# Group B's norm ahead of the output projection, z_b blocks last, and one accumulation for all 32 k-tiles

## The chip, the cores and the metric

One core of a Trainium2 chip. The metric is the device time of one launch in microseconds (us), the median of the runs shown. The engines are named as in the profile: PE is TensorE (matmuls), PEld its weight loads, DVE is VectorE, ACT ScalarE, POOL GpSimd, SP SyncE, which only issues transfers (DMAs).

## The reference: one encoder layer with two kinds of heads

256 tokens, 2048 channels, all in fp32:

```
hn = rmsnorm(x, norm_w)
q, v, f_fwd, f_bwd, z_a, b_gate, c_gate, h_b, z_b = split(hn @ w_in)        # 9 x 2048 columns
o_a = head_rmsnorm(hgrn2_forward(...) + hgrn2_backward(...)) * silu(z_a)     # group A
y_b = b_gate * conv3(c_gate * h_b)                                          # group B
o_b = rmsnorm(y_b, conv_norm_w) * silu(z_b)
h   = x + concat(o_a, o_b) @ w_out                                          # 4096 x 2048
h   = h + (p @ w_ple) * sigmoid(h @ w_ple_gate)
out = rmsnorm(h, final_norm_w)
```

The norm of o_b has one scale per token, taken from all 2048 channels of y_b. z_b is also scaled by the input norm before its silu.

## The kernel before

**Matmuls.** An fp32 product is made from two rounded halves of each operand: x = hi + lo. Three matmuls (hi·hi, hi·lo, lo·hi) give one product. Every weight block is split on the chip: ScalarE rounds it (L121), VectorE subtracts to get the rest (L122). For blocks of w_in with the tokens as moving operand, hi and lo of the activations lie side by side, and a matmul of 512 columns and one of 256 do the three (L437, L435): 64 matmuls a block, `gemm_in`.

**The weight stream.** `Stream` holds the weight blocks in the order of use. A block is loaded by SyncE into a raw buffer (three of `rawp`; from a place in w_out on, a tile named `early` is the fourth), and split into parts, each in one of five `spl` buffers. `get(i)` makes parts up to three ahead of the one asked for, with high priority. A scheduler orders each engine's instructions by priority and by when it holds them ready; all engines then run their own list in order.

**Seven products for eight.** Two pairs of output columns and two k-tiles form a 2x2 block product: eight tile products, or seven with sums of weights and sums of activations (`half`, L565 and the lines around it: `three` is one product of three matmuls). Seven need four extra PSUM banks beside the four main ones and a combination on VectorE when the banks are done. The weight sums come from one of two places. `add_own` makes them in the raw buffer with three VectorE adds (L83). `add_sums` reads them ready-made from DRAM: SyncE has copied weights to `sums` (`prepare`), and GpSimd has added to them there with accumulating transfers (L345 from w_out, then two steps L349), issued one by one at set ticks by `pumps`. A tick is a place in the matmul stream; `at(n, f)` runs f in the program n ticks later.

**Group B.** Group A takes the first half of the span. Then for i = 0..7 (256 channels each): c_gate and h_b blocks (for i = 0, 1 one by one with `gemm_in`; for i = 2, 4, 6 both columns of two i at once in `gemm_ch`, where pairs 2 and 4 of eight are seven products), then b_gate, the convolution and y_b, its square into `ysum`, then z_b, its sigmoid, the product o = y_b·silu(z_b)·conv_norm_w (without the norm's token scale) and the split into `mixb`. Late entries of group A's mixed tiles are transposed after the last z_b block (`turn(6)`, `turn(7)`), and `norm_b` gets the scale `rb` per token there: two matmuls of `ysum` against a column of ones (L1035).

**w_out.** Two halves of 1024 output columns (u = 0, 1). For each, one pass over the 16 k-tiles of group A (`mixa`) and one over the 16 of group B (`mixb`). A pass has eight pairs in the order 0, 1, 2, 3, 6, 4, 5, 7; pairs 2, 3, 4 and 5 are seven products with sums from DRAM. Each pass has its own main and extra banks (psg and psm in turn), its own combination into `hh` (which holds the residual), and the group B passes are scaled by `rb` in that addition (`add_h`). Then h is transposed (`h_transposed`) for the gate projection.

## Time and profile before

| what | before |
|---|---|
| median of 3 runs | 1108.23 us (1108.08 to 1108.48) |
| the profiled execution | 1108.31 us, span 1106.6 us |
| granted TensorE clock | 0.998 |
| DMA | 260.43 MB, mean 235 GB/s |

The profile is of one execution. Its span is a little shorter than the execution's time. A line of the timeline gives the start in us, the duration, the engine, the line of the kernel, what is written and read, and in brackets the idle time before it and what ended it. Matmuls overlap, so their pace is read from starts. An fp32 matmul that is not split shows as more than one record. A row of the table of windows gives the window, its length, the engine's busy time in it, the count, the granted clock, the DMA share and GB/s. "DMA to landing" is the time from a transfer's issue to its last byte (min/median/max of those asked for).

### The profile page before, as it was taken

The numbers are of one execution on the slowest core, as the hardware profiler recorded it, in microseconds if no ns is written. First come the engines' busy times: TensorE is split into PE (matmuls) and PEld (weight loads), VectorE is DVE, ScalarE is ACT, GpSimd is POOL, SyncE is SP. The second block draws the span as 40 slices with busy tenths as digits, with TensorE's granted clock in tenths as the row PEclk, the third lists the DMA queues.
The fourth block names the chain that finished last, engine by engine and source line by source line (L and its number), as shares of the span: only waits on it lengthen the run. The fifth ranks groups of instructions, "written<-read, shape, count | busy, mean of one in ns | idle before, by whom it ended". The sixth has DMA issues, their size and how long they took to land.

```text
span 1106.6 us, 16633 instructions
## 1 busy us (share of the span) xinstructions
PE 1096.3 (99%) x6269; PEld 936.9 (85%) x6269; DVE 892.6 (81%) x1164; ACT 685.8 (62%) x943; POOL 249.2 (23%) x203
## 2 busy tenths in 40 slices
PE   9999999999999999999999999999999999999996
PEld 8888888888888888888888888888888888888886
DVE  7798588996889778997877798789778888887673
ACT  6696577667876697575554455455447565565562
POOL 1144215205530535053430130121031000000101
PEclk9999999999999999999999999999999999999999
DMA  9886995588747874757989568577567888887542
GB/s 345 324 275 205 281 301 188 167 297 229 259 159 249 276 235 153 232 197 207 252 219 290 164 210 255 161 241 222 196 209 283 294 309 285 278 314 252 190 133 77
DMA packets 83248, 260.43 MB, mean 235 GB/s; under 512 B 8160, under 2 KB 23904, under 8 KB 68704
## 3 DMA queue, kind: packets, MB, share of 16 engines
q1 hardware_dynamic: 73920, 242.25, 62.9%
q0 software_dynamic: 8960, 16.78, 9.7%
q8 instruction: 49, 0.80, 0.3%
q10 hardware_dynamic: 288, 0.34, 0.1%
q14 instruction: 31, 0.25, 0.1%
HBM read 257.25 MB, written 35.65 MB: 265 GB/s over the span
## 4 chain that ended last, share of the span: by engine, by line
PE 98%; DVE 1%; ACT 0%; DMA 0%; issue 0%; DVEq 0%; SPq 0%; ACTq 0%
PE a L437 29%; PE a L435 15%; PE ach L565 3%; PE ach L566 3%; PE ach L564 3%; PE avz L566 3%; PE avz L564 3%; PE avz L565 3%; PE pg L1072 3%; PE pg L1073 3%; PE pg L1071 3%; PE pa L564 2%; PE pa L566 2%; PE pa L565 2%; PE a L456 1%; PE a L458 1%
## 5 line engine op out<-in xcount | busy, mean ns | idle before, releaser
L122 DVE TENSOR_TENSOR spl<-raw,spl 128x1024 fp32r<-128x1024 f32 (+2 forms) x431 | 517.5, 1215 | 132.1 <-ACT spl L121 123.9
L121 ACT CAST spl<-raw 128x1024 fp32r<-128x1024 f32 (+2 forms) x431 | 424.4, 995 | 262.8 <-PE a L435 58.8
L437 PE MATMUL a<-xs,spl 128*128 128x512 f32 x1408 | 483.8, 395 | 0.0
L435 PE MATMUL a<-xs,spl 128*128 128x256 f32 x1408 | 376.5, 278 | 0.0
L437 PEld LDWEIGHTS a<-xs,spl 128*128 128x128 f32 x1408 | 260.0, 188 | 55.4
L435 PEld LDWEIGHTS a<-xs,spl 128*128 128x128 f32 x1408 | 262.5, 188 | 5.6
L1188 POOL TENSOR_TENSOR hh<-hh,fw 128x512 f32<-128x512 f32 (+1 forms) x9 | 11.0, 1227 | 251.4 <-ACT gt L1187 248.8
L565 PE MATMUL ach<-spl,xs 128*128 128x512 f32 x156 | 60.8, 390 | 0.5 <-DVE spl L122 0.5
L564 PE MATMUL ach<-spl,xs 128*128 128x512 f32 x156 | 60.7, 389 | 0.0
L566 PE MATMUL ach<-spl,xs 128*128 128x512 f32 x156 | 60.7, 389 | 0.0
L564 PE MATMUL avz<-spl,xs 128*128 128x512 f32 x138 | 54.0, 391 | 0.0
L566 PE MATMUL avz<-spl,xs 128*128 128x512 f32 x138 | 53.7, 389 | 0.0
L565 PE MATMUL avz<-spl,xs 128*128 128x512 f32 x138 | 53.7, 389 | 0.0
L989 POOL TENSOR_TENSOR cg<-cg,bg 128x512 f32<-128x512 f32 x8 | 11.2, 1405 | 182.3 <-DVE bg L504 182.3
L503 ACT COPY r<-a 128x256 f32<-128x256 f32 x88 | 31.5, 368 | 30.3 <-PE a L435 30.2
L1071 PE MATMUL pg<-spl,ht 128*128 128x512 f32 (+1 forms) x120 | 45.2, 377 | 0.0
L737 POOL TENSOR_TENSOR qc<-pf,ge 128x256 f32<-128x256 f32 x16 | 21.0, 1316 | 107.0 <-ACT dd L727 92.1
L1072 PE MATMUL pg<-spl,ht 128*128 128x512 f32 (+1 forms) x120 | 45.0, 375 | 0.0
L1073 PE MATMUL pg<-spl,ht 128*128 128x512 f32 (+1 forms) x120 | 45.0, 375 | 0.0
L83 DVE TENSOR_TENSOR raw<-raw 128x512 f32<-128x512 f32 (+1 forms) x45 | 43.2, 959 | 0.9
L122 DVE TENSOR_TENSOR spl<-early,spl 128x1024 fp32r<-128x1024 f32 (+1 forms) x29 | 32.8, 1147 | 9.6 <-ACT spl L121 9.1
L121 ACT CAST spl<-early 128x1024 fp32r<-128x1024 f32 (+1 forms) x29 | 28.6, 990 | 18.5 <-PE pb_y L566 7.5
(378 smaller groups left out, 1893.9 us busy)
## 6 DMA issues: line engine op xcount, KB each, us to landing
raw<-in_w_in_dram SPq DMA_DIRECT2D x82, 1024.0 KB, 6.0
raw<-in_w_in_dram SPq DMA_DIRECT2D x196, 256.0 KB, 4.1
raw<-in_w_out_dram SPq DMA_DIRECT2D x36, 512.0 KB, 5.0
sums<-in_w_out_dram SPq DMA_DIRECT2D x32, 512.0 KB, 8.2
raw<-in_w_in_dram SPq DMA_DIRECT2D x26, 512.0 KB, 5.8
raw<-sums SPq DMA_DIRECT2D x13, 1024.0 KB, 5.8
raw<-in_w_gate_dram SPq DMA_DIRECT2D x9, 1024.0 KB, 5.5
sums<-in_w_out_dram POOLq DMA_DIRECT2D x16, 512.0 KB, 11.0
```

The source lines that it names most:

```text
L83: self.nc.vector.tensor_tensor(out=out, in0=out, in1=other, op=ALU.add)
L121: self.nc.scalar.copy(out=v[:, :, 0], in_=r)
L122: self.nc.vector.tensor_tensor(out=v[:, :, 1], in0=r, in1=v[:, :, 0], op=ALU.subtract)
L435: pe.matmul(a[:, :T], lhsT=lhsT, rhs=xs[:, kt, 0, :], start=False, stop=(kt == NKT - 1))
L437: pe.matmul(a, lhsT=lhsT, rhs=xs[:, kt, :, :].rearrange("p s n -> p (s n)"), start=(kt == 0), stop=False)
L503: act.copy(out=r, in_=acc[m][:, 1, :])
L564: pe.matmul(acc, lhsT=ah, rhs=w[:, 0], start=start, stop=False)
L565: pe.matmul(acc, lhsT=ah, rhs=w[:, 1], start=False, stop=False)
L566: pe.matmul(acc, lhsT=al, rhs=w[:, 0], start=False, stop=stop)
L1071: pe.matmul(acc[m], lhsT=lh, rhs=wh, start=(kt == 0), stop=False)
L1072: pe.matmul(acc[m], lhsT=lh, rhs=wl, start=False, stop=False)
L1073: pe.matmul(acc[m], lhsT=ll, rhs=wh, start=False, stop=(kt == nk - 1))
```

## The change

- w_in's blocks come in another order: c and h for i = 0, 1; b_gate of both; then for i = 2, 4, 6 the c/h pair and two b_gate blocks; and all eight z_b blocks at the end.
- y_b is kept for all i. After the last, `norm_b` runs at tick 14 of the first z_b block: two fp32 matmuls of 256 columns with a matrix of ones, so that every partition gets the scales of all tokens (`rbb`, with the reciprocal over 128x256). Each z_b block multiplies y_b by it (128x512). `mixb` is then complete, and w_out needs no scale.
- w_out adds all 32 k-tiles of a column half in the same four main and four extra banks: 16 pairs, one combination. The orders are 0, 1, 7, 2, 3, 6, 4, 5 and 0, 1, 2, 3, 6, 4, 5, 7.
- Pair 6 of each pass becomes seven products, with `add_own`.
- The accumulating transfers are issued at other ticks; the turns of group A move into the sixth z_b block; h's transposes of the first column half move to ticks 4 and 5 of the second, into psg banks.

```diff
+    def whole(c, i):
+        blocks[c, i] = sum((ws.add(w_in[c + i, h]) for h in range(2)), [])
+
     for i in range(2):
-        for c in (B_CG, B_HB, B_BG, B_ZB):
-            blocks[c, i] = sum((ws.add(w_in[c + i, h]) for h in range(2)), [])
+        for c in (B_CG, B_HB):
+            whole(c, i)
+    for i in range(2):
+        whole(B_BG, i)
     for i in range(2, 8, 2):
         blocks[B_CG, i] = []
         for q in VZ_ORDER:
@@ -206,22 +211,25 @@
             ]
             blocks[B_CG, i].append(ws.add_own(*srcs) if q in CH_SUMS else ws.add(*srcs[0], *srcs[1]))
         for ii in (i, i + 1):
-            for c in (B_BG, B_ZB):
-                blocks[c, ii] = sum((ws.add(w_in[c + ii, h]) for h in range(2)), [])
+            whole(B_BG, ii)
+    for i in range(8):
+        whole(B_ZB, i)
     first_out = len(ws.todo)
 
-    ORDER, SUMS = (0, 1, 2, 3, 6, 4, 5, 7), (2, 3, 4, 5)
+    ORDERS, SUMS, OWN = ((0, 1, 7, 2, 3, 6, 4, 5), (0, 1, 2, 3, 6, 4, 5, 7)), (2, 3, 4, 5), 6
     oblocks, prepared = [], []
     for u in range(2):
         for half in range(2):
             oblocks.append([])
-            for q in ORDER:
+            for q in ORDERS[half]:
                 k = 16 * half + 2 * q
                 srcs = [[w_out[2 * u + n, k // 4, :, k % 4 : k % 4 + 2]] for n in range(2)]
                 if q in SUMS:
                     sums = dramp.tile([P, 4, 512], F32, name=f"sums{u}_{half}_{q}")
                     prepared.append((srcs, sums))
                     oblocks[-1].append(ws.add_sums(*srcs, sums))
+                elif q == OWN:
+                    oblocks[-1].append(ws.add_own(*srcs))
                 else:
                     oblocks[-1].append(ws.add(*srcs[0], *srcs[1]))
...
+    pool.memset(wz, 1.0)
+    pumps(2, 54, 12)
+    for i in range(2):
+        cg = ctmp.tile([P, 2, T], F32, tag="cg", name=f"cg{i}", bufs=2)
+        evac(gemm_in(B_CG, i, TURNED), lambda m: cg[:, m, :], ctmp)
+        hb = ctmp.tile([P, 2, T], F32, tag="hb", name=f"hb{i}", bufs=2)
+        evac(gemm_in(B_HB, i, TURNED), lambda m: hb[:, m, :], ctmp)
+        by_norms(cg, rbc2, 2)
+        pool.tensor_tensor(out=ub[i][:, :, 1 : T + 1], in0=cg, in1=hb, op=ALU.mult)
+    bp, og, suma = kept_open()
+    for i in range(8):
+        if i > 1 and i % 2 == 0:
+            gemm_ch(i)
+            pumps(2, 18, 3)
+        hb = ctmp.tile([P, 2, T], F32, tag="hb", name=f"bg{i}", bufs=2)
+        evac(
+            gemm_in(B_BG, i, TURNED if i > 1 and i % 2 == 0 else {}), lambda m: hb[:, m, :], ctmp,
+            500 if i in (1, 3, 5) else 200,
+        )
+        convolve(i, ub[i % 2], hb)
+        if i in (0, 2, 4):
+            for z in {0: (0, 1), 2: (2,), 4: (3,)}[i]:
+                activation_sums(z, mixa)
+
+    rbb = early[:, 0:T]
+
+    def norm_b():
+        rp = psm.tile([P, 512], F32, tag="sc0", name="rp")
+        for m in range(2):
+            pe.matmul(rp[:, :T], lhsT=wz, rhs=ysum[:, m, :], start=(m == 0), stop=(m == 1))
+        dve.tensor_tensor(out=rbc2, in0=rbc, in1=rbc, op=ALU.mult)
+        dve.tensor_tensor(out=rbb, in0=rp[:, :T], in1=rbc2, op=ALU.mult)
+        act.activation(rbb, rbb, AF.Sqrt, bias=epst, scale=1.0 / D)
+        dve.reciprocal(out=rbb, in_=rbb)
+        dve.tensor_tensor(out=rbb, in0=rbb, in1=rbc, op=ALU.mult)
+
+    at(14, norm_b)
+    pumps(20, 92, 9)
+    with_own = tuple(q for q in ORDERS[0] if q in (*SUMS, OWN))
+    for i in range(8):
...
+        dve.tensor_tensor(out=cg, in0=ys[i], in1=rbb.unsqueeze(1).broadcast_to([P, 2, T]), op=ALU.mult)
+        pool.tensor_tensor(out=cg, in0=cg, in1=zb, op=ALU.mult)
+        mixb.append(bp.tile([P, 2, 2, T], F32R, tag=slot(i), name=f"mixb{i}"))
...
-    def norm_b():
-        pool.tensor_tensor(out=ysum[:, 0, :], in0=ysum[:, 0, :], in1=ysum[:, 1, :], op=ALU.add)
-        rp = psm.tile([P, 512], F32, tag="sc0", name="rp")
-        for m in range(2):
-            pe.matmul(rp[:, m : m + 1], lhsT=ysum[:, 0, m * P : (m + 1) * P], rhs=ones, start=True, stop=True)
-        dve.tensor_tensor(out=rb, in0=rp[:, 0:2], in1=rx, op=ALU.mult)
-        dve.tensor_tensor(out=rb, in0=rb, in1=rx, op=ALU.mult)
-        act.activation(rb, rb, AF.Sqrt, bias=epst, scale=1.0 / D)
-        dve.reciprocal(out=rb, in_=rb)
-        dve.tensor_tensor(out=rb, in0=rb, in1=rx, op=ALU.mult)
-
-    for e in range(2):
-        turn(6 + e, og[:, e], "yx"[e])
-    norm_b()
+        if 3 <= i < 6:
+            activation_sums(i - 3, mixb)
+        if i == 6:
+            sumo = [bp.tile([P, 4, 2, P], F32R, tag="og", name="sumo0")[:, 0:3]]
+            k = 2 * OWN
+            a = ctmp.tile([P, 2, T], F32, tag="tmp", name="sao")
+            t = ctmp.tile([P, 4, P], F32, tag="hb", name="sbo", bufs=2)
+            act_sums(mixa[:, k : k + 2], a, t)
+            act_split(sumo[0], mixa[:, k : k + 2], t)
...
+    def late_sums(dst, src):
+        s32 = tmp[:, 0].rearrange("p (o t) -> p o t", o=4)
+        act_sums(src, tmp[:, 1].rearrange("p (k t) -> p k t", k=2), s32)
+        act_split(dst, src, s32)
...
-            tag = FOUR[z + 2 * kk]
-            tp = psm.tile([P, 512], F32, tag=tag, name=f"ht{u}_{z}_{kk}")
+            place, tag = (psm, FOUR[z + 2 * kk]) if u else (psg, "g")
+            tp = place.tile([P, 512], F32, tag=tag, name=f"ht{u}_{z}_{kk}")
...
+    order = (*ORDERS[0], *(8 + q for q in ORDERS[1]))
+    which = (*with_own, *(8 + q for q in with_own))
+    for z in range(3):
+        act_split(sumb[:, z], mixb[SUMS[z]], sumb32[z])
+    at(4, lambda: late_sums(sumb[:, 3], mixb[SUMS[3]]))
+    at(10, lambda: late_sums(sumo[1], mixb[OWN]))
     for u in range(2):
         cs = [slice(512 * (2 * u + n), 512 * (2 * u + n + 1)) for n in range(2)]
 
@@ -1115,38 +1165,30 @@
                     nc.sync.dma_start(hh[:, m, 1024 * u : 1024 * u + 1024], xtok[:, m, 1024 * u : 1024 * u + 1024])
                 ),
             )
-        for src, sums, main, other, scale in ((mixa, sums_a, psg, psm, False), (mixb, sums_b, psm, psg, True)):
-            name = f"p{'ab'[scale]}{u}"
-            acc = four(main, name)
-            parts = oblocks[2 * u + scale]
-            if u == 0 and not scale:
-                for z in range(len(SUMS)):
-                    k = 2 * SUMS[z]
-                    if z == len(sumb32):
-                        sumb32.append(tmp[:, 0].rearrange("p (o t) -> p o t", o=4))
-                        act_sums(mixb[k // 2], tmp[:, 1].rearrange("p (k t) -> p k t", k=2), sumb32[z])
-                    act_split(sumb[:, z], mixb[k // 2], sumb32[z])
-            extra = lambda: four(other, "e" + name)
-            for q1, q5, q6, q7 in half([acc[0:2], acc[2:4]], extra, ORDER, SUMS, parts, src, sums, False):
-                d, v, d7, v7 = tmps
-
-                with tc.high_priority(offset=400):
-                    act.copy(out=d, in_=q1)
-                    add_h(0, cs[0], q1, scale)
-                    dve.tensor_tensor(out=d, in0=d, in1=q6, op=ALU.subtract)
-                    dve.tensor_tensor(out=v, in0=q5, in1=d, op=ALU.subtract)
-                    dve.tensor_tensor(out=d7, in0=d, in1=q7, op=ALU.subtract)
-                    dve.tensor_tensor(out=v7, in0=v, in1=q7, op=ALU.add)
-                with tc.high_priority(offset=400 if u and scale else 200):
-                    add_h(1, cs[0], d7, scale)
-                    add_h(0, cs[1], v, scale)
-                    add_h(1, cs[1], v7, scale)
-            with tc.high_priority(offset=400 if scale else 200):
-                for n in range(2):
-                    for m in range(2):
-                        add_h(m, cs[n], acc[2 * m + n], scale)
+        main, other = (psm, psg) if u else (psg, psm)
+        acc = four(main, f"p{u}")
+        parts = [*oblocks[2 * u], *oblocks[2 * u + 1]]
+        extra = lambda: four(other, f"ep{u}")
+        for q1, q5, q6, q7 in half([acc[0:2], acc[2:4]], extra, order, which, parts, mixes, all_sums, False):
+            d, v = tmp[:, 0], tmp[:, 1]
+
+            with tc.high_priority(offset=400):
+                act.copy(out=d, in_=q1)
+                add_h(0, cs[0], q1)
+                dve.tensor_tensor(out=d, in0=d, in1=q6, op=ALU.subtract)
+                dve.tensor_tensor(out=v, in0=q5, in1=d, op=ALU.subtract)
+                add_h(1, cs[0], q7, ALU.subtract)
+                add_h(1, cs[1], q7)
+            with tc.high_priority(offset=400 if u else 200):
+                add_h(1, cs[0], d)
+                add_h(0, cs[1], v)
+                add_h(1, cs[1], v)
+        with tc.high_priority(offset=400):
+            for n in range(2):
+                for m in range(2):
+                    add_h(m, cs[n], acc[2 * m + n])
         for z in range(2):
-            at(5 + 2 * z, lambda u=u, z=z: h_transposed(u, z))
+            at(5 + 2 * z if u else 4 + z, lambda u=u, z=z: h_transposed(u, z))
```

Three places show how rows move. First TensorE from the last z_b block (`a_7`) into w_out: `pa` and `p` are the main banks 0 to 3, `ogt` the turns, `rp` the norm. Before:

```order
L435 MATMUL a_7_1_7686<-xs,spl_7687 128x256
L679 MATMUL ogt_7783<-ident,og 128x128 x4
L679 MATMUL ogt_7792<-ident,og 128x128 x4
L1035 MATMUL rp<-ones,ysum 128x1 x2
L564 MATMUL pa_0_7822<-spl_7709,mixa 128x512
...
L564 MATMUL pa_2_7824<-spl_7709,mixa 128x512
```

Now:

```order
L443 MATMUL a_7_1_7740<-xs,spl_7741 128x256
L572 MATMUL p_0_7865<-spl_7763,mixa 128x512
...
L572 MATMUL p_2_7867<-spl_7763,mixa 128x512
...
L572 MATMUL p_2_7867<-spl_7782,mixa 128x512
L572 MATMUL p_3_7868<-spl_7763,mixa 128x512
```

The turns and the norm stand elsewhere; the second k-tile's first four products (spl_7782, three for bank 0 and the first for bank 2) now come ahead of the first product in bank 3.

Then GpSimd around the first c/h pair: L345 and L353 are the accumulating transfers from w_out, L349 and L357 those inside `sums`; `y_1`, `y_2` are the squares of y_b 1 and 2, `cg_5983` and `yb_5787` y_b 2, after the pair. Before:

```order
L1004 TENSOR_TENSOR cg_5186<-cg_5186,zb_5470 128x512
L345 DMA sums_1_4_95<-in_w_out_dram 256x1x512
L345 DMA sums_1_5_96<-in_w_out_dram 256x1x512
L349 DMA sums_0_2_89<-sums_0_2_89 128x512
L989 TENSOR_TENSOR cg_5983<-cg_5983,bg_5879 128x512
L992 TENSOR_TENSOR ysum<-ysum,y_2_5991 128x512
```

Now:

```order
L1008 TENSOR_TENSOR ysum<-ysum,y_1_5376 128x512
L353 DMA sums_1_4_95<-in_w_out_dram 256x1x512
L353 DMA sums_1_5_96<-in_w_out_dram 256x1x512
L1005 TENSOR_TENSOR yb_5787<-yb_5787,bg_5684 128x512
L1008 TENSOR_TENSOR ysum<-ysum,y_2_5795 128x512
L357 DMA sums_0_2_89<-sums_0_2_89 128x512
```

Two transfers stand ahead of the pair instead of three; the first L357 is behind y_b 2.

Last, VectorE around pair 6 of the first pass of w_out. Before, spl330 and spl331 are its two halves:

```order
L122 TENSOR_TENSOR spl329_7956<-raw149_7945,spl329_7956 128x2x512
L122 TENSOR_TENSOR spl330_7968<-raw150_7965,spl330_7968 128x1024
L122 TENSOR_TENSOR spl331_7974<-raw150_7965,spl331_7974 128x1024
L122 TENSOR_TENSOR spl332_7985<-early_152,spl332_7985 128x2x512
L122 TENSOR_TENSOR spl333_7994<-early_152,spl333_7994 128x512
```

Now spl332 and spl333 are its first two parts of four:

```order
L122 TENSOR_TENSOR spl331_8029<-raw150_8018,spl331_8029 128x2x512
L122 TENSOR_TENSOR spl332_8040<-early_152,spl332_8040 128x2x512
L122 TENSOR_TENSOR spl333_8046<-early_152,spl333_8046 128x512
L83 TENSOR_TENSOR early_152<-early_152 128x2x512
L83 TENSOR_TENSOR early_152<-early_152 128x512 x2
```

The three adds L83 stand between the second and the third part.

More of the change, by code (lines that the diff above doesn't have):

```diff
@@ L960, in gemm_ch, with kept_open @@
         at(12, lambda: convolved(i, a))
-    for i in range(8):
-        u = ub[i % 2]
-        if i < 2:
-            pumps(2, 52, 6)
-            cg = ctmp.tile([P, 2, T], F32, tag="cg", name=f"cg{i}", bufs=2)
-            evac(gemm_in(B_CG, i, {} if i else TURNED), lambda m: cg[:, m, :], ctmp)
-            hb = ctmp.tile([P, 2, T], F32, tag="hb", name=f"hb{i}", bufs=2)
-            evac(gemm_in(B_HB, i, {} if i else TURNED), lambda m: hb[:, m, :], ctmp)
-            by_norms(cg, rbc2, 2)
-            pool.tensor_tensor(out=u[:, :, 1 : T + 1], in0=cg, in1=hb, op=ALU.mult)
-        elif i % 2 == 0:
-            gemm_ch(i)
-        if i >= 2 and i % 2 == 0:
-            pumps(2, 37, 6)
-        kick = {} if i % 2 else TURNED
-        hb = ctmp.tile([P, 2, T], F32, tag="hb", name=f"bg{i}", bufs=2)
-        evac(gemm_in(B_BG, i, kick), lambda m: hb[:, m, :], ctmp)
-        if i >= 2:
-            cg = ctmp.tile([P, 2, T], F32, tag="cg", name=f"cg{i}", bufs=2)
+    def kept_open():
+        assert kept
+        actx.close()
+        bp = mctx.enter_context(tc.tile_pool(name="bp", bufs=1, side="right", reuse_waits="tile"))
+        og = bp.tile([P, 2, 2, 2, P], F32, tag="og", name="og")
+        for e in range(2):
+            act.copy(out=og[:, e], in_=kept[e])
+        return bp, og, bp.tile([P, len(SUMS), 3, 2, P], F32R, name="suma")
@@ new lines, in slot, with activation_sums, convolve @@
+    def slot(i):
+        return f"mix{i}" if i < 6 else f"late{i - 6}"
+    def activation_sums(z, src):
+        k = 2 * SUMS[z]
+        a = ctmp.tile([P, 2, T], F32, tag="tmp", name=f"sa{z}_{src is mixa}")
+        if src is mixa:
+            t = ctmp.tile([P, 4, P], F32, tag="hb", name=f"sb{z}", bufs=2)
+            act_sums(mixa[:, k : k + 2], a, t)
+            act_split(suma[:, z], mixa[:, k : k + 2], t)
+        else:
+            act_sums(mixb[k // 2], a, sumb32[z])
+    ys = []
+    def convolve(i, u, hb):
+        y = bp.tile([P, 2, 2, T], F32, tag=slot(i), name=f"yb{i}")[:, 0]
@@ L988, in tile_hymba_encoder @@
                 )
[L989 removed]
+        pool.tensor_tensor(out=y, in0=y, in1=hb, op=ALU.mult)
         y2 = ctmp.tile([P, 2, T], F32, tag="tmp", name=f"y2_{i}")
[L991 removed]
+        act.activation(y2, y, AF.Square)
         pool.tensor_tensor(out=ysum, in0=ysum, in1=y2, op=ALU.add)
[L993 to L994 removed]
@@ L996, in tile_hymba_encoder @@
+    at(14, norm_b)
+    pumps(20, 92, 9)
+    with_own = tuple(q for q in ORDERS[0] if q in (*SUMS, OWN))
+    for i in range(8):
+        if i == 5:
+            for e in range(2):
+                at(2, lambda e=e: turn(6 + e, og[:, e], "yx"[e]))
+        zb = ctmp.tile([P, 2, T], F32, tag="hb", name=f"zb{i}", bufs=2)
+        evac(gemm_in(B_ZB, i, TURNED if i in (1, 6) else {}), lambda m: zb[:, m, :], ctmp)
+        by_norms(zb, rbc, 2)
         sz = ctmp.tile([P, 2, T], F32, tag="tmp", name=f"szb{i}")
-        act.activation(sz, hb, AF.Sigmoid)
+        act.activation(sz, zb, AF.Sigmoid)
@@ L1060, in tile_hymba_encoder @@
     sums_a, sums_b = ([t[:, z] for z in range(len(SUMS))] for t in (suma, sumb))
-    tmps = [*(tmp[:, b] for b in range(2)), *(og[:, e].rearrange("p m h t -> p (m h t)") for e in range(2))]
+    sumo.append(spare.tile([P, 3, 2, P], F32R, name="sumo1"))
+    all_sums = []
+    for half_sums, o in zip((suma, sumb), sumo):
+        part = [half_sums[:, z] for z in range(len(SUMS))]
+        part.insert(with_own.index(OWN), o)
+        all_sums += part
+    mixes = [*(mixa[:, 2 * k : 2 * k + 2] for k in range(8)), *mixb]
+    def late_sums(dst, src):
+        s32 = tmp[:, 0].rearrange("p (o t) -> p o t", o=4)
+        act_sums(src, tmp[:, 1].rearrange("p (k t) -> p k t", k=2), s32)
+        act_split(dst, src, s32)
     def gemm_tok(acc, ids, lhs, todo=((0, slice(0, 512)), (1, slice(0, 512)))):
```

45 lines of the change are left out of this document (9 added, 36 removed).

## The prediction

> **What bounds the kernel now.** I read the head of the page first, then the chain of work that ended last:
>
> ```profile
> span 1106.6 us, 16633 instructions
> PE 1096.3 (99%) x6269; PEld 936.9 (85%) x6269; DVE 892.6 (81%) x1164; ACT 685.8 (62%) x943; POOL 249.2 (23%) x203
> PE 98%; DVE 1%; ACT 0%; DMA 0%; issue 0%; DVEq 0%; SPq 0%; ACTq 0%
> ```
>
> TensorE is the bound, and 98% of the chain is its own instructions. A busy share does not show stalls, so the list of TensorE's waits comes next:
>
> ```profile
> PE wps L272 <- DVE wz L267: 1.1, 1, 1.1
> PE ach L565 <- DVE spl L122: 0.5, 1, 0.5
> ```
>
> Two waits in the whole kernel: one at the start, which the change leaves alone, one in group B. So the time is the number of matmuls times their spacing, and the change can win by fewer matmuls or by that one wait, and lose by any new one. The spacing is taken from starts on the timeline, because durations overlap:
>
> ```profile
> 1029.71 0.39 PE L1072 MATMUL pg<-spl,ht 128*128 128x512 f32 x1
> ...
> 1034.47 0.39 PE L1072 MATMUL pg<-spl,ht 128*128 128x512 f32 x1
> ```
>
> 21 spacings lie between these starts, (1034.47 - 1029.71) / 21 = 0.227 us per 128x512 matmul.
>
> **1. Matmuls removed.** w_out has four passes (two column halves u, each with 16 k-tiles of group A and 16 of group B). A plain pair of k-tiles is 8 products of three matmuls, a seven-product pair 7. One more pair per pass turns to seven: 4 x 3 = 12 matmuls fewer, which the program's counts confirm (3811 to 3799 of 128x512). 12 x 0.227 = **-2.72 us**. [...]
>
> **2. Where w_out starts.** Its third and fourth bank are those of the last z_b block. Before, ten small matmuls stood between:
>
> ```profile
> 830.43 1.04 PE L679 MATMUL ogt<-ident,og 128*128 128x128 f32 x8
> 830.69 0.42 DVE L504 TENSOR_TENSOR zb<-a,r 128x256 f32<-128x256 f32 x1 [0.47 <-ACT r L503]
> 831.31 0.50 PE L1035 MATMUL rp<-ones,ysum 128*128 128x1 f32 x4
> 831.67 0.48 PE L564 MATMUL pa<-spl,mixa 128*128 128x512 f32 x1
> 833.10 0.42 DVE L504 TENSOR_TENSOR zb<-a,r 128x256 f32<-128x256 f32 x1
> ```
>
> Banks came free 0.68 and 3.09 us after z_b's end at 830.43. In the change no turn stands between (TensorE's order above, p_3 pushed back). Bank p_2 is wanted after 3 matmuls (0.68 us), p_3 after 13 (2.95). Both arrive at about that moment: 0 to 0.3, I take **+0.1**. The turns moved, their eight matmuls are paid elsewhere.
>
> **3. The norm of group B.** Before, two one-column matmuls L1035 give a scale per token after the last z_b block: 831.67 - 831.31 = 0.36 us in the rows above. Now two fp32 matmuls of 256 columns against ones give it to all partitions, inside the first z_b block. The nearest rows are two fp32 matmuls of 128 columns, in group A:
>
> ```profile
> 49.93 0.60 PE L412 MATMUL rps<-ident,rw 128*128 128x128 f32 x4
> 50.29 0.48 PE L437 MATMUL a<-xs,spl 128*128 128x512 f32 x1
> 50.60 0.28 PE L435 MATMUL a<-xs,spl 128*128 128x256 f32 x1
> ```
>
> They show as four records, hold TensorE for 0.36 us and lengthen the spacing behind them from 0.23 to 0.31: 0.44, as one column does. Twice the columns cost from 0.44 to 0.88, 0 to +0.44 over the old pair. I take **+0.4**, the dear end, as the columns of all larger matmuls here cost in proportion. The wait ahead of them: ysum must be ready some 9.7 us into that block, where the matmuls stand in TensorE's order.
>
> ```profile
> 819.34 0.39 PE L437 MATMUL a<-xs,spl 128*128 128x512 f32 x1
> ...
> 824.30 1.49 POOL L992 TENSOR_TENSOR ysum<-ysum,y 128x512 f32<-128x512 f32 x1 [0.74 <-ACT y L991]
> ```
>
> The last y block of before ended at 819.34 and POOL's last addition 6.5 us later: 3 us of cover, cost 0 (if it were late, all of z_b's first block would wait, 1 us for 1 us). The reciprocal over 256 columns, the product of y and scale (128x512) in each z_b block, and the two turns moved into the sixth z_b block take VectorE's time; a z_b block has 11.1 us:
>
> ```profile
> 819.30:830.40 11.10, 6.83 (x8) 1.00 0.48 170
> ```
>
> 6.83 us of VectorE in the last z_b block of before; 0.7 more for the product and 2 to 3 for activation sums or turns in some blocks makes 8 to 11. TensorE's stream hides it: cost 0, and each us over 11.1 would cost about one. Combination adds that w_out has fewer were off the path: no gain.
>
> **4. The wait at the first c/h pair.** With z_b last, the two y blocks precede this pair, and POOL's queue changes. As its order above shows, three accumulating transfers ahead of the pair's loads become two; the third moves behind the pair (L345 moves 512 KB into DRAM with an addition, L349 256 KB).
>
> ```profile
> 572.61 1.60 POOL L1004 TENSOR_TENSOR cg<-cg,zb 128x512 f32<-128x512 f32 x1 [3.15 <-DMA raw<-in_w_in_dram]
> 574.15 2.11 POOL L345 DMA_DIRECT2D sums<-in_w_out_dram  x2
> 575.28 1.83 POOL L349 DMA_DIRECT2D sums<-sums  x1
> ```
>
> Beside them the pair's loads L100, issued from 578 to 584, took long to land; those of the second c/h pair, issued from 666 to 672, did not (the first and the second row):
>
> ```profile
> DMA to landing us min/median/max: 7.8/10.5/11.0
> DMA to landing us min/median/max: 5.3/5.9/6.5
> ```
>
> And the wait behind the late load:
>
> ```profile
> 591.41 1.05 ACT L121 CAST spl<-raw 128x1024 fp32r<-128x1024 f32 x1 [4.06 <-DMA raw<-in_w_in_dram]
> 592.50 1.23 DVE L122 TENSOR_TENSOR spl<-raw,spl 128x1024 fp32r<-128x1024 f32 x1 [3.88 <-DMA raw<-in_w_in_dram]
> 592.90 0.39 PE L564 MATMUL ach<-spl,xs 128*128 128x512 f32 x1
> 593.78 0.50 PE L565 MATMUL ach<-spl,xs 128*128 128x512 f32 x1 [0.49 <-DVE spl L122]
> 594.11 0.39 PE L566 MATMUL ach<-spl,xs 128*128 128x512 f32 x1
> ```
>
> From 592.90 to 594.11 two spacings take 1.21 instead of 0.45 us: 0.76 lost. A landing 0.8 us earlier cures it, and the transfer that moved landed last of the three. Between 0 and -0.76; I take **-0.76**.
>
> **5. Pair 6 of each pass.** Its weight sums are now made by VectorE in SBUF. In VectorE's order above three adds come between second and third part. A part's lead over TensorE is set by the five split buffers, not by VectorE:
>
> ```profile
> 862.63 1.05 ACT L121 CAST spl<-early 128x1024 fp32r<-128x1024 f32 x1 [0.30 <-PE epa_x L566]
> ...
> 863.71 1.23 DVE L122 TENSOR_TENSOR spl<-early,spl 128x1024 fp32r<-128x1024 f32 x1
> ...
> 867.19 0.39 PE L564 MATMUL pa<-spl,mixa 128*128 128x512 f32 x1
> ```
>
> This part is split at 863.71 + 1.23 and used 2.25 us later. What the adds take is shown by a c/h pair, which has the same code:
>
> ```profile
> 757.60 1.82 DVE L122 TENSOR_TENSOR spl<-raw,spl 128x1024 fp32r<-128x1024 f32 x2
> 759.34 2.67 DVE L83 TENSOR_TENSOR raw<-raw 128x1024 f32<-128x1024 f32 x3
> 761.93 1.22 DVE L122 TENSOR_TENSOR spl<-raw,spl 128x1024 fp32r<-128x1024 f32 x1
> ```
>
> With N the pair's first matmul: part one is done at N - 2.25, so begun at N - 3.47; adds 1.74 later, N - 1.73; part three 2.59 after that, N + 0.86, done N + 2.08. TensorE wants it after nine matmuls, N + 2.04: 0.1 us late with the hand-over. Behind it stand part four, done N + 3.2 and wanted N + 3.4, and the next pair's first part, done N + 4.4 and wanted N + 4.8: no further wait. Four passes: **+0.4** (0 to 0.8; late activation sums stand before the first).
>
> What is late next is the sums' transfer two pairs on: it reuses pair 6's raw buffer. That is free when part four is split, 1.14 after part three, at N + 3.2. The part that needs the sums is used two pairs later (21 x 0.227 = 4.77 each), at N + 9.54 + 2.04 = N + 11.6; cast and split take 2.4 of that (593.78 - 591.41 above). The transfer has 11.6 - 2.4 - 3.2 = 5.9 us, about.
>
> ```profile
> DMA to landing us min/median/max: 4.7/6.3/9.2
> DMA to landing us min/median/max: 4.9/4.9/4.9
> DMA to landing us min/median/max: 7.1/7.1/7.1
> ```
>
> These are all fifteen such transfers of w_out, then the one issued at 886.6 and the one at 866.7 alone. In SyncE's order the load ahead of the new one left nearly 7 us earlier (its buffer is freed by the split of the part before pair 6), so it starts on idle engines; I take 4.9 to 5.9, **0**. At 7.1 it is 1.2 per pass.
>
> **6. Between the halves of columns.** h's transposes of the first half come at ticks 4 and 5 instead of 5 and 7, in other banks. Up to the last add that they need, VectorE's order has six splits of 1.14 us, one of 0.6 and nine 128x512 operations of 0.6 (the two pitches of the 1.74 above), 12.8 us. They begin when the first bank's last product is done, nine matmuls or 2.0 us before the second half, 1.4 with a split ahead; so they end 10.8 to 11.4 into it, and the last transposes stand behind 52 matmuls' time, 11.8. **+0.2** (0 to 1).
>
> **Sum.** -2.72 + 0.1 + 0.4 - 0.76 + 0.4 + 0.2 = -2.38. Profiled time 1108.31 (span 1106.6 and 1.7 around it), 0.08 above the median 1108.23; 1108.23 - 2.38 = **1105.9 us**. About 0.2% (2.2 us, 1106.0) can be told from no change, so this forecast lies at that edge.
>
> **Rivals.** *Clean:* no new wait, 1108.23 - 2.72 + 0.4 - 0.76 = 1105.2. For it: no wait in w_out now. Against: the margins of 0.1 us under 2 and 5. *Joints:* the terms 2, 4, 5 and 6 go to their dear ends (0.2 + 0.76 + 0.4 + 0.8 more): 1108.0, or 1106.9 for half of it. For it: the margins there are 0.4 us and less. *The sums land late, slower:* at 7.1 us, 4 x 1.2 = +4.8, 1110.7; it decides from 6.5 us, where 4 x 0.6 eats the 2.4. For it: the median is 6.3, and five pairs now load 8 MB in 23.9 us. Against: the two quiet loads of 4.8 to 4.9. That the change doesn't do what it says is excluded by the counts.
>
> **Chances.** Forecast 0.50 (1105.3 to 1106.7; 0.32 of it under 1106.0), clean 0.13, joints 0.20, late sums 0.17 (0.15 beyond 1110.4). Faster 0.32 + 0.13 = 0.45; slower 0.15 + 0.01 = 0.16; same the rest, 0.39. The range goes from clean less 0.2, 1105.0, to 1109.6, halfway into late sums.
>
> **What would show it.** No wait in the first c/h pair; TensorE's waits name the third part of pair 6 with some 0.1 us each and no part of sums; the first thirteen matmuls of w_out take 2.95 us. I am wrong if TensorE waits on a split after pair 6 for more than 0.5 us, or if a z_b block exceeds 11.1 us.

## The result, and the profile after

The changed kernel takes **1123.61 us** (median of 4 runs, 1123.04 to 1124.70). The kernel before takes 1108.17 beside it; the ratio is 1.0140, with a 95% interval of 1.0122 to 1.0158. The forecast was 1105.9 with a range to 1109.6: the change is 15.4 us slower. The profiled execution took 1123.04 us.

The head of the page and TensorE's list of waits, of the changed kernel (us in total, times, longest):

```profile
span 1121.3 us, 16655 instructions
PE 1099.5 (98%) x6257; PEld 934.3 (83%) x6257; DVE 897.1 (80%) x1182; ACT 684.7 (61%) x951; POOL 253.2 (23%) x203
PE p L572 <- DVE zb L512: 6.4, 1, 6.4
PE ach L572 <- DVE bg L512: 1.7, 1, 1.7
PE avz L572 <- DVE qt L512: 1.5, 1, 1.5
PE wps L280 <- DVE wz L275: 1.1, 1, 1.1
PE p_sc L572 <- ACT spl L121: 1.0, 1, 1.0
PE p_sc L573 <- DVE spl L122: 0.8, 1, 0.8
PE ogt L687 <- DVE ogz L677: 0.4, 1, 0.4
PE p L573 <- DVE spl L122: 0.3, 1, 0.3
```

The twelve matmuls are gone, and TensorE's busy time rose by 3.2 us all the same. Before, the list had two entries; now it has eight. The old wait at a c/h pair (L565) is not among them, but there are new waits in four places.

**The start of w_out** is the largest. TensorE's timeline there (start, duration):

```profile
838.15 0.39 PE L574 MATMUL p<-spl,mixa 128*128 128x512 f32 x1
844.96 0.80 PE L572 MATMUL p<-spl,mixa 128*128 128x512 f32 x1 [6.42 <-DVE zb L512]
845.55 0.63 PE L573 MATMUL p<-spl,mixa 128*128 128x512 f32 x1
...
847.25 0.63 PE L574 MATMUL p<-spl,mixa 128*128 128x512 f32 x1
```

Six matmuls of w_out run, and the seventh needs the banks of the last z_b block, which VectorE empties at 844.49: 844.96 - 838.15 = 6.81 us for one spacing of 0.227, so 6.58 lost. The next ones start 0.42 us apart, (847.25 - 845.55) / 4 = 0.425. The table of windows (the eighth column is the granted clock) shows why:

```profile
838.40:844.90 6.50, 0.14 (x1) 0.00 (x0) 6.43 (x12) 3.77 (x7) 1.68 (x1) 0.71 0.16 46
845.50:848.20 2.70, 2.70 (x8) 2.15 (x7) 0.87 (x2) 0.38 (x1) 1.27 (x1) 0.55 0.90 370
848.30:851.00 2.70, 2.70 (x13) 2.22 (x12) 1.88 (x3) 1.35 (x3) 1.30 (x1) 1.00 0.41 167
```

After the idle stretch the granted clock is 0.55 from 845.50 to 848.20 and 1.00 from 848.30. The ten matmuls from 844.96 to 848.50 take 3.54 us from first to last start where nine spacings of 0.227 make 2.04: 1.5 us more. So this place costs 8.1 us (the expectations below reckon with 1.7 and 8.3). A busy share hides the second part: TensorE is busy for all 2.70 us of the row at 0.55.

**Why the banks are late.** A z_b block takes TensorE 11.1 us. VectorE falls behind from block to block. One late block, in the timelines of VectorE, GpSimd and ScalarE, then three blocks in the table of windows (VectorE's busy time is the fifth entry), and a row of VectorE's list of waits:

```profile
821.19 0.41 DVE L512 TENSOR_TENSOR zb<-a,r 128x256 f32<-128x256 f32 x1
821.52 1.21 DVE L122 TENSOR_TENSOR spl<-raw,spl 128x1024 fp32r<-128x1024 f32 x1
824.58 0.88 DVE L1061 SCALAR_TENSOR_TENSOR zb<-zb,vec,szb 128x256 f32<-128x256 f32 x2 [1.85 <-ACT szb L1058]
821.68 2.20 POOL L516 TENSOR_TENSOR zb<-zb,rbc 128x512 f32<-128x512 f32 x1 [6.22 <-DVE zb L512]
823.91 0.63 ACT L1058 ACTIVATE szb<-zb 128x512 f32<-128x512 f32 x1 [3.22 <-POOL zb L516]
784.40:795.74 11.34, 11.34 (x67) 9.99 (x67) 7.56 (x11) 5.72 (x9) 5.24 (x3) 1.00 0.79 226
808.59:821.19 12.60, 12.60 (x73) 10.95 (x73) 11.76 (x21) 7.69 (x12) 4.63 (x4) 1.00 0.58 155
821.19:834.03 12.84, 12.84 (x76) 11.23 (x75) 10.23 (x17) 5.85 (x9) 3.91 (x2) 1.00 0.64 221
DVE zb L1061 <- ACT szb L1058: 12.0, 7, 2.1
```

VectorE empties the second bank (821.19), does one split, and then stands in its own order before the product L1061. That needs ScalarE's sigmoid, which needs GpSimd's product by the norms. VectorE works 10.23 us in the 12.84 from one second bank to the next: its work fits into TensorE's 11.1, its work and its waits don't. (Only the block with the two turns, 11.76, has more work than that.) Seven such waits make 12.0 us. Before, where z_b blocks alternated with b_gate blocks, two such waits (L1000 is the product there, L997 the sigmoid) made 1.0 us:

```profile
DVE zb L1000 <- ACT szb L997: 1.0, 2, 0.7
```

GpSimd's instruction is also slower than before. Its groups (sum, mean ns), before and after (each x8):

```profile
L508 POOL TENSOR_TENSOR zb<-zb,rbc 128x512 f32<-128x512 f32 x8 | 10.4, 1300 | 42.6 <-DVE zb L504 42.6
```

```profile
L516 POOL TENSOR_TENSOR zb<-zb,rbc 128x512 f32<-128x512 f32 x8 | 15.1, 1886 | 45.8 <-DVE zb L512 45.8
```

The difference goes with which of the two begins first. Before, GpSimd began ahead of VectorE's next split in seven of the eight blocks, and it was the split that took longer, 1.93 us instead of the usual 1.22 where it began 0.45 us behind:

```profile
568.16 1.30 POOL L508 TENSOR_TENSOR zb<-zb,rbc 128x512 f32<-128x512 f32 x1 [3.92 <-DVE zb L504]
568.61 1.93 DVE L122 TENSOR_TENSOR spl<-raw,spl 128x1024 fp32r<-128x1024 f32 x1 [0.53 <-ACT spl L121]
```

In the late block of the changed kernel above, the split begins first (821.52 to 822.73), and GpSimd's product, begun at 821.68, takes 2.20 us instead of 1.30: 0.9 us more, about what is left of the split when it starts (822.73 - 821.68 = 1.05 us).

**Group A.** GpSimd's timeline there:

```profile
267.95 3.35 POOL L357 DMA_DIRECT2D sums<-sums  x4
286.29 0.81 POOL L357 DMA_DIRECT2D sums<-sums  x1 [14.99 <-DMA sums<-sums]
286.83 1.58 POOL L516 TENSOR_TENSOR qt<-qt,rbc 128x512 f32<-128x512 f32 x1
```

The program issues this second step of a weight sum in group B. The scheduler put it into group A, ahead of a product by the norms, and there it waits 15 us for the first step to land. The product comes at 286.83 instead of 281.36, and TensorE loses 0.56 us at 300 and 1.71 at 318 behind it.

**The first c/h pair** loses 1.81 us at 552.04: its banks come from b_gate's second block, and VectorE empties them after two sets of activation sums.

**The seams behind five seven-product pairs** lose 3.3 us in all (at 886, 921, 924 and, most of it, 970 and 971). Pair 6 holds its raw buffer until its last part is split, and meanwhile no load runs; then several leave together. Windows (the ninth column is the DMA share) and SyncE's issues:

```profile
955.00:958.00 3.00, 3.00 (x15) 2.44 (x14) 2.94 (x4) 2.60 (x5) 0.00 (x0) 1.00 0.00 1
959.50:966.50 7.00, 7.00 (x32) 5.82 (x31) 6.47 (x7) 3.97 (x5) 0.00 (x0) 1.00 0.89 272
957.89 0.33 SPq L96 DMA_DIRECT2D early<-sums  x1
959.63 3.76 SPq L100 DMA_DIRECT2D raw<-in_w_out_dram  x4
```

**The books.** Losses 2.3 (group A), 1.8 (c/h), 8.1 (start of w_out), 3.3 (seams), 0.4 (at 1015.85, behind the second half's transposes of h) and 0.4 (the norm's matmuls), less 2.7 for the twelve matmuls and 0.8 for the old c/h wait: 12.8. The span grew by 1121.3 - 1106.6 = 14.7; the other 1.9 us are small delays that I did not assign.

### The profile page after: what moved, and what is told of

Read it like the earlier page. It is cut to its first block, busy times and chain, and to the rows that moved or that the text cites. A ratio compares the mean times of both kernels' runs of the same rounds, so it can differ in the third digit from the quotient of the medians.

```text
span 1121.3 us, 16655 instructions
## 1 busy us (share of the span) xinstructions
PE 1099.5 (98%) x6257; PEld 934.3 (83%) x6257; DVE 897.1 (80%) x1182; ACT 684.7 (61%) x951; POOL 253.2 (23%) x203
## 4 chain that ended last, share of the span: by engine, by line
PE 74%; DVE 10%; DMA 5%; POOL 4%; ACT 3%; issue 2%; SPq 0%; DVEq 0%; ACTq 0%; POOLq 0%
PE a L445 20%; PE a L443 10%; DVE spl L122 5%; PE ach L572 3%; PE ach L573 3%; PE ach L574 3%; PE avz L572 3%; PE avz L574 3%; PE avz L573 3%; PE pg L1119 2%; PE pg L1120 2%; PE pg L1118 2%; ACT spl L121 2%; DMA sums<-sums 2%; DMA raw<-in_w_out_dram 1%
## 5 line engine op out<-in xcount | busy, mean ns | idle before, releaser
L121 ACT CAST spl<-raw 128x1024 fp32r<-128x1024 f32 (+2 forms) x435 | 423.5, 991 | 236.2 <-DVE raw L83 53.6
L445 PE MATMUL a<-xs,spl 128*128 128x512 f32 x1408 | 485.4, 395 | 0.0
L445 PEld LDWEIGHTS a<-xs,spl 128*128 128x128 f32 x1408 | 260.1, 188 | 55.5
L1230 POOL TENSOR_TENSOR hh<-hh,fw 128x512 f32<-128x512 f32 (+1 forms) x9 | 11.1, 1243 | 253.9 <-ACT gt L1229 251.3
L1005 POOL TENSOR_TENSOR yb<-yb,bg 128x512 f32<-128x512 f32 x8 | 13.5, 1682 | 184.6 <-DVE bg L512 136.2
L83 DVE TENSOR_TENSOR raw<-raw 128x512 f32<-128x512 f32 (+1 forms) x51 | 49.7, 974 | 1.2
L121 ACT CAST spl<-early 128x1024 fp32r<-128x1024 f32 (+1 forms) x33 | 31.9, 984 | 29.4 <-PE pg L1120 7.6
L122 DVE TENSOR_TENSOR spl<-early,spl 128x1024 fp32r<-128x1024 f32 (+1 forms) x33 | 37.0, 1139 | 14.0 <-ACT spl L121 13.7
```

The lines of the kernel that those rows point to most:

```text
L83: self.nc.vector.tensor_tensor(out=out, in0=out, in1=other, op=ALU.add)
L121: self.nc.scalar.copy(out=v[:, :, 0], in_=r)
L122: self.nc.vector.tensor_tensor(out=v[:, :, 1], in0=r, in1=v[:, :, 0], op=ALU.subtract)
L445: pe.matmul(a, lhsT=lhsT, rhs=xs[:, kt, :, :].rearrange("p s n -> p (s n)"), start=(kt == 0), stop=False)
```

## The experiments

The kernel before measured 1108.3 to 1108.7 beside them. Theory and rivals were formed in turn; the first theory of the 8.1 us is not the one that stood. Each single mend ran twice, and its two times lie 0.1 to 2.5 us apart, so for prices of 1 to 3 us the waits in the traces say more than the times. One source of the spread is the start: in six of the fourteen profiled executions of these experiments TensorE waits 0.5 to 1.5 us within the first 10 us, for a weight block (`PE a L445 <- ACT spl L121`). No edit touches that place, and the profiles of the kernel before and of the changed kernel have no such wait.

### Group A: issue the sums two ticks later

```diff
-    pumps(2, 54, 12)
+    pumps(4, 54, 12)
```

> The change with one number altered: the twelve accumulating transfers at the start of group B are due from tick 4 instead of tick 2, after which the first of them stands in group B again in GpSimd's order and no longer ahead of a group A product. Theory (GpSimd's queue): that transfer waited from 269.6 to 286.3 us for an earlier one and held the product behind it, so TensorE's two waits in group A (0.56 and 1.71 us before 319) go and the time falls by 2.3 to 2.7, to 1121.0. Rival (the waits in group A come from slower landings in that execution): they stay, 1123.6. The other waits are not touched in either.

Measured: 1121.68 us (1120.42 to 1122.94). Both waits of group A are gone, and the product by the norms starts at 281.73 again:

```profile
281.73 1.29 POOL L516 TENSOR_TENSOR qt<-qt,rbc 128x512 f32<-128x512 f32 x1 [10.11 <-DVE gx L730]
```

So the 2.3 us are the hoisted transfer. Part came back elsewhere: the wait at the first c/h pair grew from 1.7 to 2.4 us, and the clock dropped to 0.51 behind it.

### c/h: one set of activation sums between a gate's blocks

```diff
-        if i in (0, 2, 4):
-            for z in {0: (0, 1), 2: (2,), 4: (3,)}[i]:
-                activation_sums(z, mixa)
+        if i in (0, 2, 4, 6):
+            activation_sums(i // 2, mixa)
```

> The change with the activation sums of group A spread over the b_gate blocks 0, 2, 4 and 6, one set each, instead of two sets behind block 0. Theory (VectorE empties the banks of b_gate block 1 late because two sets of sums, and a wait for GpSimd's ysum, stand ahead of it): the wait at the first c/h pair (1.8 us near 552) goes, 1121.8. Rival (the banks are late because of the split or the load ahead): 1.5 us or more of it stay, 1123.6.

Measured: 1122.48 us (1121.58 to 1123.39); the time overlaps that of the changed kernel, but the loss at 552 falls from 1.81 to 0.22 us. VectorE's other wait there, 3.2 us for GpSimd's addition to `ysum` ahead of the first set, is still in the trace. So the second set was the cause.

### Seams: other orders, and pair 6 plain

Three runs: the first pass in the second's order; orders in which plain pairs stand among the seven-product ones; pair 6 with eight products, as before the change.

```diff
-    ORDERS = ((0, 1, 7, 2, 3, 6, 4, 5), (0, 1, 2, 3, 6, 4, 5, 7))
+    ORDERS = ((0, 1, 2, 3, 6, 4, 5, 7), (0, 1, 2, 3, 6, 4, 5, 7))     # run 1
+    ORDERS = ((0, 1, 2, 3, 7, 6, 4, 5), (0, 2, 3, 1, 6, 4, 5, 7))     # run 2
...
-                elif q == OWN:                                         # run 3, with its sums of activations
-                    oblocks[-1].append(ws.add_own(*srcs))
```

> The change with the order of pairs of the first pass as before (0, 1, 2, 3, 6, 4, 5, 7), so that a plain pair stands again between the five seven-product pairs and the next pass. Theory (loads bunch behind pair 6 and the next pass needs two raw buffers at once): the two waits at the start of the second pass of the second half (1.1 and 1.0 us near 970) and the 0.6 near 886 go, 1123.6 - 2.7 = 1120.9. Rival (pair 6's own adds make VectorE late, wherever the plain pair stands): 2 us or more of waits remain, now inside or right behind the five pairs, 1123 to 1124.

> The change with w_out's pairs in the orders 0, 1, 2, 3, 7, 6, 4, 5 and 0, 2, 3, 1, 6, 4, 5, 7: a plain pair splits the run of five seven-product pairs, nothing else. Theory (raw buffers: pair 6 holds its buffer until its last split, so no load leaves for some 3 us, then four leave together and land after 7 to 10 us): with less demand in a row the 3.2 us of waits behind the runs (near 886, 921 and 970) fall under 1, 1120.6. Rival (VectorE's adds alone make the next parts late): the same 2 to 3 us turn up behind pair 6, 1123.

> The change with pair 6 of each pass undone: eight products again, no adds, no activation sums for it (12 matmuls more, 2.65 us of VectorE less in the seventh z_b block and as much less in w_out). The rest as in the change. If pair 6 causes the waits behind the runs of pairs, these 3.2 us go; the wait at the start of w_out loses what the sums added, 1.9 of 6.4. 1123.6 + 2.7 - 3.2 - 1.9 = 1121.2. If the joined passes cause them (no plain pair ahead of the second pass), they stay: 1124.4.

Measured: run 1 1124.64 us (1124.07 to 1125.22), the waits only moved to other seams. Run 2 1122.43 (1121.56 to 1123.30), run 3 1121.75 (1121.68 to 1121.82): in both no wait for a split is left in w_out. Run 2's time shows less than the 3.3 us that went, because its profiled execution waits 1.3 us at the start of the kernel. Run 3 has the twelve matmuls back (+2.7) and is still 1.9 us below the changed kernel, 1.0 of it at w_out's start, where the wait is 5.4. So the seams are pair 6's held buffer in a run of five, and what it costs is set by where the plain pairs stand.

### z_b: product and mixed block later in the order

The sigmoid, the product L1061 and the mixed block of z_b's blocks are put 6, 8 and 13 ticks later, then 10, 14 and 22.

```diff
-        act.activation(sz, zb, AF.Sigmoid)
...
+        for dt, fn in zip((10, 14, 22) if i < 6 else (10, 14, 15), (sigmoid, product, mixed)):
+            if i < 7:
+                at(dt, fn)
```

> The change with the same work in each z_b block, but sigmoid, product and split of a block pinned 6, 8 and 13 ticks into the next block in ScalarE's and VectorE's order (the last block as it was). Theory A (order: VectorE and ScalarE stand idle in line for sigmoid and product, 1.85 us each time, so that 7.7 us of work take over 11.1): the drift goes, TensorE's wait for the banks at the start of w_out falls from 6.4 to under 1 us and the halved pace behind it (7 matmuls at 0.43 us) goes too, 1123.6 - 7.5 = 1116. Theory B (amount: VectorE has simply too much to do in the z_b blocks): the wait stays over 4 us, 1121 to 1124.

> The first attempt to move the z_b blocks' tails left VectorE's order as it was (one split between the emptied banks and the product), so it decided nothing. Here sigmoid, product and split of a block are pinned 10, 14 and 22 ticks behind it, and two splits stand between the second emptied bank and the product. The same work, another order. Theory A (order: waits in line make VectorE late): TensorE's wait for banks at the start of w_out falls from 6.4 to under 1.5 us, 1123.6 - 7 = 1116.6. Theory B (amount: VectorE's work in the z_b blocks is over 11.1 us): the wait stays over 4 us.

Measured: 1123.36 us (1122.48 to 1124.25), wait 6.5: VectorE's order hardly changed, so it decides nothing. With 10, 14, 22: 1120.56 (1119.47 to 1121.64), wait 3.9, between the two expectations (under 1.5, over 4). The first blocks now come 11.09 us apart, those with activation sums still 12 to 13. I took the rest for VectorE's amount of work. That it is not amount alone, the next runs show.

### The four mends together

> The four mends together: transfers due from tick 4, one set of activation sums per b_gate block, the z_b tails 10, 14 and 22 ticks later, and pair orders 0, 1, 2, 3, 7, 6, 4, 5 and 0, 2, 3, 1, 6, 4, 5, 7. If the four causes are separate, their prices add: 1123.6 - 2.6 - 2.0 - 8.3 - 3.4 = 1107.3, about 0.1% under the kernel before, of which the removed matmuls are the gain. If they share VectorE as one cause, part of the waits turns up elsewhere and it stays over 1110.

Measured: 1115.08 us (1114.68 to 1116.01), ratio 1.0061 (1.0044 to 1.0077). The wait of 3.9 is left, with 2.2 us of slow clock behind it (0.85 on average from 837 to 860), and two of about 0.9 in w_out. A late z_b block of this kernel, in the timelines of GpSimd, ScalarE and VectorE (its line numbers differ from the changed kernel's: the sigmoid is L1061 here):

```profile
814.35 3.62 POOL L516 TENSOR_TENSOR zb<-zb,rbc 128x512 f32<-128x512 f32 x1 [3.77 <-DVE zb L512]
818.00 0.63 ACT L1061 ACTIVATE szb<-zb 128x512 f32<-128x512 f32 x1 [2.95 <-POOL zb L516]
814.19 0.68 DVE L1082 TENSOR_TENSOR mixb<-ob,mixb 128x512 fp32r<-128x512 f32 x1
815.60 1.22 DVE L122 TENSOR_TENSOR spl<-raw,spl 128x1024 fp32r<-128x1024 f32 x1
819.60 1.23 DVE L122 TENSOR_TENSOR spl<-raw,spl 128x1024 fp32r<-128x1024 f32 x1 [2.79 <-ACT spl L121]
```

VectorE works without a gap from 814.19 to 816.82; GpSimd's instruction, which takes 1.30 us where it begins first, ends 1.15 us after that. ScalarE stands in its sigmoid meanwhile, with the cast for the next split behind it, and VectorE waits 2.79 us for that cast. It is the same chain, which now ends in another wait.

### Amount or chain: take work off VectorE

The late sums go to GpSimd (1.8 us a set off VectorE); in the second run also the product of y with the norm.

```diff
-            act_sums(mixb[k // 2], a, sumb32[z])
+            act_sums(mixb[k // 2], a, sumb32[z], eng=pool)     # so for the other two late callers
-            dve.tensor_tensor(out=cg, in0=ys[i], in1=rbb..., op=ALU.mult)
+            pool.tensor_tensor(out=cg, in0=ys[i], in1=rbb..., op=ALU.mult)     # second run only
```

> The four mended parts of the run before (the seven-product pairs spread, the earlier loads of group B, one set of activation sums between a gate's blocks, the later ticks of the z_b blocks), and beside them every set of the late sums, of the attention's sums and of the mixed blocks' sums on GpSimd in place of VectorE. Theory (amount: in z_b's blocks with activation sums VectorE has 12 to 13 us of work and waits for 11.09 us of TensorE): the blocks come 11.1 to 11.5 us apart again, TensorE's wait for the emptied banks at w_out's start falls from 3.9 to under 1 us and the slow pace behind it goes, so 1115.1 - 3.9 - 2.2 + 1 = about 1110 us or less. Rival (order: VectorE is late because of what its products and mixed blocks wait for on ScalarE and GpSimd): the wait stays above 3 us, and 1114 to 1117 us, more if GpSimd's sums delay its own products by the norms.

> The run before, and beside it the product of y with the norm (one per z_b block) on GpSimd too, which takes another row of VectorE's away in every block. Theory (amount): if any wait is left at w_out's start it shrinks further, by up to some 0.6 us a block, and the time is equal to the run before or up to 2 us below it. Rival (GpSimd's turn sets the blocks): GpSimd's own product by the norms starts later, the sigmoid behind it too, and the wait is the same or longer than in the run before.

Measured: 1123.68 us (1122.38 to 1125.61) and 1124.42 (1123.94 to 1124.51), about 9 us slower than the four mends. TensorE's wait and a row of VectorE's, first run:

```profile
PE p L572 <- DVE zb L512: 11.0, 1, 11.0
818.80 0.29 DVE L568 TENSOR_TENSOR mixb<-early,mixb 128x128 fp32r<-128x128 f32 x1 [4.68 <-ACT mixb L567]
```

VectorE has less to do and is later. From 756 to 838 it is busy 61.0 us instead of 70.4 with the four mends; but in blocks 4 to 6 it stands 3.4 to 4.7 us before the little split L568 of those sums, which now hangs on GpSimd through ScalarE. The runs took work off VectorE and put it into a chain that VectorE waits for, so they do not price the amount by itself. They do show that VectorE can be late without being full.

### The chain, made shorter with more work for VectorE

The product by the norms of z_b goes from GpSimd to VectorE: 0.7 us a block more for VectorE. The other run leaves the engines as they are and puts the sigmoid behind two of ScalarE's casts. Both stand on the four mends.

```diff
-        by_norms(zb, rbc, 2)
+        by_norms(zb, rbc, 2, dve)
```

```diff
-        for dt, fn in zip((10, 14, 22) if i < 6 else (10, 14, 15), (sigmoid, product, mixed)):
+        for dt, fn in zip((13, 17, 25) if i < 6 else (10, 14, 15), (sigmoid, product, mixed)):
```

> The four mended parts together (1115.08 us), and beside them z_b's product by the norms on VectorE in place of GpSimd, in all eight blocks. It adds about 0.7 us of work a block to VectorE and takes from the chain emptied bank, product by the norms, sigmoid, ScalarE's next split casts, VectorE's next split the GpSimd instruction, which took 3.62 us in two of the late blocks where VectorE worked beside it. Theory (chain): the sigmoid starts sooner, VectorE's wait of 2.79 us for a split of ScalarE behind the sigmoid goes, the blocks with sums come 11.1 to 12 us apart in place of 12.1 to 13.1, TensorE's wait for the emptied banks at w_out's start falls from 3.9 to under 2 us: 1110 to 1113 us. Rival (amount: VectorE's own work in the blocks with sums is what is too long): 0.7 us more in each block, the wait grows to 5 to 8 us, 1116 to 1120 us.

> The four mended parts together (1115.08 us), with the sigmoid, the product and the mixed block of z_b's blocks 0 to 5 three ticks later again (13, 17, 25 in place of 10, 14, 22), so that on ScalarE the casts of the next two splits stand ahead of the sigmoid; amounts as they were on every engine. Theory (chain): ScalarE no longer stands in its sigmoid while VectorE waits for a cast, the blocks with sums come 11.1 to 12 us apart, the wait at w_out's start falls under 2 us: 1109 to 1113 us. Rival (amount): the work is the same, the wait stays above 3 us: 1114 to 1117 us.

Measured, first: **1109.45 us** (10 runs, 1108.00 to 1110.67), ratio 1.0007 (0.9997 to 1.0017), 5.6 us less than without it. TensorE's whole list of waits:

```profile
PE wps L280 <- DVE wz L275: 1.1, 1, 1.1
PE p L573 <- DVE spl L122: 0.8, 1, 0.8
PE p L572 <- DVE zb L512: 0.6, 2, 0.4
PE ach L572 <- DVE bg L512: 0.4, 1, 0.4
```

Adding work to VectorE took the waits at the emptied banks from 3.9 to 0.6: the chain decides. Second: 1115.45 (1112.21 to 1116.43). The wait fell to 2.0, as the chain has it, but a new one of 2.5 us for a cast came at 859 in w_out (granted clock of the whole execution 0.994, against 0.997 in the first run). The time is the rival's. The late cast had itself stood 4.7 us for a weight load; why that load was late stays open.

### The chain alone, in the changed kernel

The same line as above, and nothing else, in the changed kernel; and beside it the five mends with the product of y and norm on GpSimd.

> The changed kernel with one thing other: z_b's product by the norms on VectorE in place of GpSimd, in all eight blocks. Theory (the chain emptied bank, GpSimd's product, sigmoid, VectorE's product, with GpSimd's instruction slow beside VectorE, is by itself the cause of the wait at w_out's start): although VectorE has 0.7 us more to do in each block, the wait of 6.4 us falls to under 2 us, the slow pace behind it goes (1.7 us), and all else stays: 1123.6 - 4.4 - 1.7 = about 1117.5 us or less, 1115 to 1118. Rival (the chain only matters together with the later ticks, which put splits ahead of the product): the wait stays over 4 us, 1121 us or more.

> The four mended parts and the product by the norms on VectorE (1109.45 us), and the product of y with group B's norm on GpSimd in place of VectorE (0.7 us a block off VectorE, off the chain). Theory (with the chain short VectorE's amount is no longer above TensorE's in any block but by tenths): the 0.9 us at w_out's start may fall by some tenths, 1108.5 to 1109.5 us. Rival (amount is still the bound of the blocks with sums): all 0.9 us goes and loads leave sooner in w_out's first pass, 1106.5 to 1108 us, below the kernel before.

Measured: **1115.78 us** (1114.59 to 1117.36), ratio to before 1.0063 (1.0049 to 1.0077). One line takes back 7.8 of the 15.4 us. TensorE's wait at the start of w_out, and then VectorE's order in a late block:

```profile
PE p L572 <- DVE zb L512: 1.0, 1, 1.0
819.60 0.41 DVE L512 TENSOR_TENSOR zb<-a,r 128x256 f32<-128x256 f32 x1
...
820.14 0.68 DVE L516 TENSOR_TENSOR zb<-zb,rbc 128x512 f32<-128x512 f32 x1
820.74 1.21 DVE L122 TENSOR_TENSOR spl<-raw,spl 128x1024 fp32r<-128x1024 f32 x1
821.88 0.87 DVE L1061 SCALAR_TENSOR_TENSOR zb<-zb,vec,szb 128x256 f32<-128x256 f32 x2
```

Bank to product now takes 821.88 - 820.01 = 1.87 us instead of 824.58 - 821.60 = 2.98, and the sigmoid is done before VectorE asks for it: its waits for the sigmoid fall from 12.0 to 0.8 us in all. The amount of work still counts: VectorE is busy 11.9 of 12.0 us in the block with the turns and 10.9 to 11.0 of 11.7 to 12.2 in its neighbours, and a wait of 1.0 us is left.

The second run: 1108.95 (11 runs, 1108.43 to 1110.15), ratio 1.0004 (0.9995 to 1.0013); the waits for banks make 0.8 us, so with the chain short 0.7 us less on VectorE buys nothing there. No version was faster than the kernel before: with nearly every new wait mended the change is worth nothing that can be measured. The removed matmuls and the old c/h wait are worth 3.5 us; in the profile of the last run 1.3 us are lost at the start of w_out, 0.9 before a split at 876 and 0.4 at the norm's matmuls. The rest of the missing gain is not assigned.

## Why the prediction was wrong

- **Term 3 is the step that failed** ("TensorE's stream hides it: cost 0"). It added up VectorE's busy time in a z_b block, 8 to 11 us, and the trace has 7.6 to 11.8. But VectorE, with its list in fixed order, also stands: 12.0 us in seven of the blocks, mostly 1.85 at a time, behind GpSimd and ScalarE. I had even given a price for a block over 11.1 us, and tested it against work alone; late blocks came 12.6 to 12.8 us apart, which the prediction had named as a sign that it is wrong. TensorE waited 6.4 us for VectorE after eight such blocks. That b_gate blocks between them would have let VectorE catch up is likely, but no run put them back. GpSimd's product, up to 2.3 us here against 1.30 before, is in no term.
- **Term 2** (+0.1) rested on banks being emptied as promptly as before. TensorE lost 6.6 us there, and the clock of 0.55 behind the wait, 1.5 us, was in no rival. The reading that p_2 is wanted after 3 matmuls was wrong as well: six run before the wait. That error made the term dearer, not cheaper.
- **Term 4** was right in its own place: the old wait (0.76) is gone. The moved sums of activations made a new one of 1.81 in front of the first pair. I looked at GpSimd's order there, and not at VectorE's.
- **Group A** was in no term. I compared GpSimd's order only around group B, where the transfers are issued in the program. The scheduler had moved one across, 15 us of waiting.
- **Term 5** put +0.4 on the third part of pair 6, and nothing on the sums' transfer. Neither made a wait (the transfer issued at 957.89 took 4.9 us to land), so the term was 0.4 too dear in its own place. The step missed is one further: the loads behind it, which left together after an empty stretch and took up to 9.8 us to land. That is 3.3 us in place of 0.4.
- **The norm's matmuls** and the one behind them take from 755.91 to 757.00, 1.09 us; less 0.23 for that one, 0.86. Over the 0.44 of the old pair that is 0.4, as forecast.

```profile
755.91 1.03 PE L1040 MATMUL rp<-ysum,wz 128*128 128x256 f32 x4
756.59 0.58 PE L445 MATMUL a<-xs,spl 128*128 128x512 f32 x1
757.00 0.28 PE L443 MATMUL a<-xs,spl 128*128 128x256 f32 x1
```

- **Term 6** (+0.2): TensorE's list names no wait for the first half's transposes. The 0.4 in the books is behind those of the second half.
- **Term 1** held: twelve matmuls fewer at 0.227 us.

The rival on the slower side had the sums' transfer, at 1110.7: the right neighbourhood, the wrong transfer, and far too small.
